# A hybrid Mamba-2 and attention step on Trainium2: operand parts tied behind the newest weight part

## The chip, the cores and the metric

The kernel runs on one core of a Trainium2 chip (trn2). The metric is the device time of one execution in microseconds (us). TensorE (PE) multiplies, VectorE (DVE), ScalarE (ACT) and GpSimd (POOL) do the elementwise work, and SyncE (SP) issues the DMAs between the memory of the chip and the on-chip buffers. Products are accumulated in PSUM banks and read from there by DVE or ACT.

## What is computed

The reference is one inference step of a two-layer decoder trunk. Eight sampled sequences of 8 tokens, one prompt of 1024 tokens and 16 meta tokens go through it together, 1104 columns in all; after the first layer the meta tokens are dropped and 1088 columns remain. Cut to what matters here:

```python
def sq_relu_mlp(h, norm_w, w_up, w_down):
    return h + jnp.square(jax.nn.relu(rmsnorm(h, norm_w) @ w_up)) @ w_down

# layer 0
out = gated_group_rmsnorm(y, z, gate_w) @ w_out      # the output product of the Mamba-2 mixer
h = h + out
h = sq_relu_mlp(h, mlp_norm_w[0], w_up[0], w_down[0])
# layer 1
h = h + swa(queries(h), shared keys and values) @ w_o
h = sq_relu_mlp(h, mlp_norm_w[1], w_up[1], w_down[1])
y = rmsnorm(h, final_norm_w)
```

The model is 1024 wide, the mixer's inner width is 2048 and the MLP's is 4096. All of it is float32.

## The kernel before

**Split operands.** A float32 product is made of three matmuls in the type fp32r (`mm3`, L205 to L207): high part of the weight by high part of the operand, high by low, and low by high. So every operand of PE is first split in two parts: ACT writes the high part with a cast, then DVE writes the low part as a difference. A pair of such instructions is called parts below. There are three places that make them in the stages of this case:

- `wparts` (L1051) makes weight parts. It takes a tile from a ring of six (`wtile`, tag w), casts on ACT (L1053) and subtracts on DVE (L1054). Its source is a weight block as loaded (raw) or a sum of such blocks (s), made on DVE (L1172 and L1178 in the output and down products, L1063 and L1069 in the up product).
- `parts` in `side_io` (L1223) makes the parts of one side, an operand of a product set, in place: ACT L1235, DVE L1236. The tiles are pieces of the big buffers S and R and a few of their own called A.
- `block_parts` (L1148) makes a quarter of the parts of a plain block, the buffer R0 (tile R): ACT L1151, DVE L1152.

**The stages.** The output product (in the trace from about 850 to 985 us), the up product and the down product of each layer (up 1100 to 1380 us and 2225 to 2505 us, down 1437 to 1699 us and 2560 to 2819 us) use a scheme of seven products in place of eight for 2 by 2 blocks. The mixer and the attention lie before and between them and are not touched.

**block_products (L1239)** runs the output product in 2 blocks and each down product in 4. In a block it takes four sets p = 0 to 3, and in a set seven products i = 0 to 6. One product is 18 matmuls of 128 x 276 columns (272 in layer 1) into one of four PSUM banks ma, mb, mc, md, in the order that CHAIN gives (`"adcbacd"` in even sets, `"abcdacb"` in odd ones). The products of a set accumulate on one another in their banks, and after each of the seven an eviction on DVE (L1270) adds the bank to one of the tiles us and hh; the first set's first is a copy on ACT (L1289). A bank can be written anew only when its eviction has read it, and a weight tile of the ring only when the product that used it six weights before is done. In the last block of a stage three more additions of us to hh follow (L1294), two of them on POOL and one on DVE.

The nested `step(b, p, i)`, called after each product, loads and splits the operands to come: the first two sides of block b + 1 after product 2 of sets 1 and 2, the other five at the positions that `make` lists, from set 3 into set 0 of the next block, and in the last block the four quarters of the plain block, after product 2 of sets 1, 2 and 3 and product 5 of set 3 (`last[1]`, which is `block_parts`). The stage then ends with a plain block product that reads R0.

**up (L1123)** runs 14 pairs f = 2 to 15 of the up product (`up_pair`) with weights from `up_weights` and sides that are made once at its start; it loads R0 at f = 8 and splits its quarters after f = 12 to 15, for the plain block with which the down product begins.

**What sets the order.** The order in which the code is traced is not the order on the engines. A scheduler places each engine's instructions by a simulated time, under the data dependences; it may put an instruction that was traced late ahead of one traced before it on the same engine. The context manager `tc.issue_after(ins)` adds an edge that only orders: what is traced inside it stands behind `ins` on the engine of `ins`. The kernel before uses it in two places, behind the newest load of weights (`last_raw`; one is `load_stream`, L1139).

Of the kernel before, what the change touches and what calls it, by code (L numbers as in the profile page):

```python
# [3 lines left out]

# [5 lines left out]
F32 = mybir.dt.float32  # L10
F32R = mybir.dt.float32r
AF = mybir.ActivationFunctionType
ALU = mybir.AluOpType
# [81 lines left out]
class Stream:  # L95
# [29 lines left out]
    def load(self, X):  # L125

        self.X = X
        for c in self.rs:
            self.k.nc.sync.dma_start(out=X[:, :, self.cols(c)], in_=self.h_d[:, :, self.cols(c)])
        for c in list(self.rs):  # L130
            self.norm(c)
# [11 lines left out]
class Kernel:  # L143
# [906 lines left out]
    def wparts(self, src, shape):  # L1050
        nc = self.nc  # L1051
        t = self.wtile([P, 2] + shape)
        nc.scalar.copy(out=t[:, 0], in_=src)  # L1053
        nc.vector.tensor_tensor(out=t[:, 1], in0=src, in1=t[:, 0].bitcast(F32), op=ALU.subtract)  # L1054
        return t[:, 0], t[:, 1]

    def up_weights(self, layer, f):
# [90 lines left out]
    def block_parts(self, j, buf):  # L1148
        nc = self.nc
        hi, lo = buf[:, 0, j], buf[:, 1, j]  # L1150
        nc.scalar.copy(out=hi, in_=lo.bitcast(F32))  # L1151
        nc.vector.tensor_tensor(out=lo, in0=lo.bitcast(F32), in1=hi.bitcast(F32), op=ALU.subtract)  # L1152

    def down_block(self, layer, b, buf, hts, chs, tail=0, done=None, step=None):

# [83 lines left out]
    def block_products(self, w, big, us, slots, load, parts, free, make, last, more, early=(0, 0), w0=None):  # L1239


        nc = self.nc
        nn = us.shape[2]
        qw = nn // 2
        nb = len(slots)
        h = [[big[:, 4 * j:4 * j + 4, i * nn:i * nn + nn] for i in range(2)] for j in range(2)]

        def step(b, p, i):

            if b == nb - 1:  # L1250
                if (p, i) == (0, 0):
                    last[0]()
                if p > 0 and i == 2:
                    last[1](p - 1)
                if p == 3 and i == 5:
                    last[1](3)
            else:
                for k in range(2):
                    if i == 0 and p == early[k]:
                        load(b + 1, k)  # L1260
                if p in (1, 2) and i == 2:
                    parts(b + 1, p - 1)
                if p == 3 and i in free[b]:
                    load(b + 1, free[b].index(i) + 2)
                if p == 3 and i in make[b]:
                    parts(b + 1, make[b].index(i) + 2)
            if p == 0 and b and i + 7 in make[b - 1]:
                parts(b, make[b - 1].index(i + 7) + 2)

        tt = lambda out, x, y: nc.vector.tensor_tensor(out=out, in0=x, in1=y, op=ALU.add)  # L1270
        for b in range(nb):
            for p in range(4):
                banks = {}
                hv = [[h[j][i][:, p] for i in range(2)] for j in range(2)]
                uv = us[:, p]
                for i, (wh, wl) in enumerate(w0 if w0 is not None and (b, p) == (0, 0) else self.down_weights(w[b], p)):
                    e = self.CHAIN[p % 2][i]
                    new = e not in banks
                    if new:
                        banks[e] = self.pq.tile([P, 1024], F32, tag=e, bufs=1, name="m" + e)  # L1280
                    x = [(hi[:, q], lo[:, q]) for hi, lo in slots[b][i] for q in range(lo.shape[1])]
                    for k in range(2):
                        cs = slice(k * qw, k * qw + qw)
                        self.mm3(banks[e][:, 512 + (k - 1) * qw:512 + k * qw], [(wh[:, q], wl[:, q]) for q in range(KB)],
                                 [(hi[:, cs], lo[:, cs]) for hi, lo in x], new)
                    pv = banks[e][:, 512 - qw:512 + qw]
                    to = (uv, hv[1][1], hv[1][1], uv, hv[0][0], hv[1][0], hv[0][1])[i]
                    if i == 0 and b == 0:
                        nc.scalar.copy(out=uv, in_=pv)  # L1289
                    else:  # L1290
                        tt(to, pv, to)
                    if b == nb - 1 and i in (3, 4, 5):
                        e, to = ((nc.gpsimd, hv[1][1]), (nc.gpsimd, hv[0][1]), (nc.vector, hv[1][0]))[i - 3]
                        e.tensor_tensor(out=to, in0=to, in1=uv, op=ALU.add)  # L1294
                    step(b, p, i)
                    more(b, p, i)
# [736 lines left out]
```

## Time and profile before

| | us |
|---|---|
| median of 3 runs | 2892.56 |
| the runs | 2887.66, 2892.56, 2895.99 |
| the profiled execution, its own time | 2889.1 |
| its span, first to last instruction | 2887.0 |
| mean granted clock of PE | 0.991 |

| engine | busy us | share of the span |
|---|---|---|
| PE | 2805.9 | 97% |
| DVE | 2084.4 | 72% |
| ACT | 1417.7 | 49% |
| POOL | 465.4 | 16% |

A line of the trace names the engine, the line of the program, the operation and the tiles, out<-in. The name of a tile leaves out its buffer number, so `w<-s,w` is the low part of a weight made of a sum and its high part, `S<-S` or `A<-A` are side parts, `R<-R` are plain parts at L1152 and side parts at L1236, and `us<-ma,us` is an eviction of the bank ma. DVE's instructions overlap a little at their ends: a row of 0.55 us may be followed 0.47 us after its start.

Matmuls of one product follow one another without a gap when nothing is waited for, so a stretch of PE shows its losses in two ways: as waits with a releaser, and as fewer matmuls in a stretch than in a quiet one of the same length. Where the granted clock is below 1.00, matmuls are slower too.

### The profile page before, as it was taken

What the parts mean: (1) busy time and instruction counts of PE and PEld (TensorE: products, weight loads), DVE (VectorE), ACT (ScalarE), POOL (GpSimd) and SP (SyncE); (2) the same over time, 40 slices, a digit from 0 to 9 for tenths busy, and PEclk for the clock granted to TensorE, in tenths of its full rate; (3) what the DMA queues carried; (4) which work ended last, traced back from release to release, by engine and by line L of the source; (5) the groups of instructions that cost most, each with busy time, mean ns of one, the idle gap of its engine ahead of it and who ended that gap; (6) DMA issues with size and microseconds to landing.
All of it is one profiled execution on the core that took longest, in us unless ns stands there. A gap on an engine that the chain in (4) does not pass through costs nothing.

```text
span 2887.0 us, 51424 instructions
## 1 busy us (share of the span) xinstructions
PE 2805.9 (97%) x19895; PEld 2700.3 (94%) x19895; DVE 2084.4 (72%) x3615; ACT 1417.7 (49%) x2742; POOL 465.4 (16%) x659
## 2 busy tenths in 40 slices
PE   8999999989999999999999999999999999999997
PEld 6999999979989999999999999888989999999997
DVE  6788888876778686665677875676688666567786
ACT  6555555555654275454343336556555454523333
POOL 3255555551100100000000022110110000000011
PEclk9999999999999999999999999999999999999999
DMA  4244444457654225343645423456553444624431
GB/s 138 83 128 124 123 123 126 129 134 259 247 200 162 93 92 175 128 149 142 250 171 188 163 94 103 162 170 235 184 191 126 138 146 147 231 101 132 146 102 69
DMA packets 219467, 433.41 MB, mean 150 GB/s; under 512 B 30728, under 2 KB 128392, under 8 KB 216648
## 3 DMA queue, kind: packets, MB, share of 16 engines
q1 hardware_dynamic: 219224, 430.14, 44.9%
q8 instruction: 156, 2.56, 0.4%
q14 instruction: 87, 0.71, 0.1%
HBM read 302.71 MB, written 128.32 MB: 149 GB/s over the span
## 4 chain that ended last, share of the span: by engine, by line
PE 82%; DVE 8%; DMA 4%; ACT 2%; issue 2%; POOL 0%; SPq 0%; DVEq 0%; ACTq 0%; POOLq 0%
PE g L205 11%; PE g L206 11%; PE g L207 11%; PE mc L205 4%; PE mc L207 4%; PE mc L206 4%; PE ma L205 3%; PE ma L206 3%; PE ma L207 3%; PE md L206 3%; PE md L207 3%; PE md L205 3%; PE mb L205 3%; PE mb L207 3%; PE mb L206 3%
## 5 line engine op out<-in xcount | busy, mean ns | idle before, releaser
L206 PE MATMUL g<-S,w 128*128 128x384 f32 (+2 forms) x1584 | 531.6, 336 | 0.0
L205 PE MATMUL g<-S,w 128*128 128x384 f32 (+2 forms) x1584 | 529.8, 335 | 1.9 <-DMA w<-ws_q 0.7
L207 PE MATMUL g<-S,w 128*128 128x384 f32 (+2 forms) x1584 | 527.4, 333 | 0.0
L1053 ACT CAST w<-s 128x384 fp32r<-128x384 f32 (+1 forms) x272 | 150.4, 557 | 346.4 <-DVE s L1178 85.3
L205 PEld LDWEIGHTS g<-S,w 128*128 128x128 f32 x1584 | 298.7, 189 | 4.5 <-issue 1.2
L206 PEld LDWEIGHTS g<-S,w 128*128 128x128 f32 x1584 | 298.8, 189 | 3.0 <-issue 2.4
L207 PEld LDWEIGHTS g<-S,w 128*128 128x128 f32 x1584 | 299.4, 189 | 2.2 <-issue 1.7
L1294 POOL TENSOR_TENSOR hh<-hh,us 128x552 f32<-128x552 f32 (+1 forms) x24 | 36.3, 1532 | 1563.4 <-DVE us L1270 1563.4
L205 PE MATMUL ma<-S,w 128*128 128x276 f32 (+1 forms) x808 | 234.7, 291 | 5.9 <-DVE us L1270 4.4
L207 PE MATMUL ma<-S,w 128*128 128x276 f32 (+1 forms) x808 | 234.4, 290 | 0.0
L206 PE MATMUL ma<-S,w 128*128 128x276 f32 (+1 forms) x808 | 234.0, 290 | 0.0
L1054 DVE TENSOR_TENSOR w<-s,w 128x384 fp32r<-128x384 f32 (+1 forms) x272 | 167.1, 619 | 69.3 <-ACT w L1053 69.2
L1053 ACT CAST w<-raw 128x384 fp32r<-128x384 f32 (+1 forms) x204 | 111.8, 556 | 162.7 <-PE mc L207 47.2
L171 ACT CAST w<-raw 128x1024 fp32r<-128x1024 f32 x96 | 100.6, 1048 | 133.6 <-PE g L206 49.0
L205 PEld LDWEIGHTS ma<-S,w 128*128 128x128 f32 x808 | 153.1, 189 | 7.2 <-ACT w L1053 3.6
L206 PE MATMUL g<-R,w 128*128 128x384 f32 (+2 forms) x480 | 158.3, 330 | 0.0
L205 PE MATMUL g<-R,w 128*128 128x384 f32 (+2 forms) x480 | 157.8, 329 | 0.0
L207 PE MATMUL g<-R,w 128*128 128x384 f32 (+2 forms) x480 | 157.7, 329 | 0.0
L172 DVE TENSOR_TENSOR w<-raw,w 128x1024 fp32r<-128x1024 f32 x96 | 122.6, 1277 | 43.9 <-ACT w L171 29.3
L206 PEld LDWEIGHTS ma<-S,w 128*128 128x128 f32 x808 | 153.2, 190 | 0.1
L207 PEld LDWEIGHTS ma<-S,w 128*128 128x128 f32 x808 | 152.9, 189 | 0.0
L205 PE MATMUL mc<-S,w 128*128 128x276 f32 (+1 forms) x512 | 148.1, 289 | 0.3 <-DVE hh L1270 0.3
(491 smaller groups left out, 8568.4 us busy)
## 6 DMA issues: line engine op xcount, KB each, us to landing
raw<-in_w_up_dram SPq DMA_DIRECT2D x64, 512.0 KB
raw<-in_w_in_dram SPq DMA_DIRECT2D x48, 512.0 KB
raw<-in_w_downs_dram SPq DMA_DIRECT2D x64, 384.0 KB
w<-ws_o SPq DMA_DIRECT2D x48, 512.0 KB
w<-ws_q SPq DMA_DIRECT2D x40, 512.0 KB
ab<-acs_d SPq DMA_DIRECT2D x64, 256.0 KB
S<-t_d SPq DMA_DIRECT2D x18, 828.0 KB
S<-t_e SPq DMA_DIRECT2D x18, 816.0 KB
```

Source lines behind the costliest of these rows:

```text
L171: nc.scalar.copy(out=wh, in_=raw)
L172: nc.vector.tensor_tensor(out=wl, in0=raw, in1=wh.bitcast(F32), op=ALU.subtract)
L205: mm(out=out, lhsT=wh, rhs=xh, start=(first and k == 0), stop=False)
L206: mm(out=out, lhsT=wh, rhs=xl, start=False, stop=False)
L207: mm(out=out, lhsT=wl, rhs=xh, start=False, stop=(k == n - 1))
L1053: nc.scalar.copy(out=t[:, 0], in_=src)
L1054: nc.vector.tensor_tensor(out=t[:, 1], in0=src, in1=t[:, 0].bitcast(F32), op=ALU.subtract)
L1294: e.tensor_tensor(out=to, in0=to, in1=uv, op=ALU.add)
```

## The change

`wparts` now keeps its two instructions as `last_hi` (ACT) and `last_lo` (DVE), those of the newest weight parts traced. A new context manager `behind` opens `issue_after` on both. `block_parts` always works inside it, and so do the three calls of `parts` in the `step` of `block_products`. So each of these operand parts stands, on ACT and on DVE, behind the weight parts that were traced last before it. The calls of `parts` outside `step` (in `gates_out`, and in `first` of `down_blocks`) are left as they were. No instruction is added, taken away or given other data.

```diff
-        nc.scalar.copy(out=t[:, 0], in_=src)
-        nc.vector.tensor_tensor(out=t[:, 1], in0=src, in1=t[:, 0].bitcast(F32), op=ALU.subtract)
+        self.last_hi = nc.scalar.copy(out=t[:, 0], in_=src).ins
+        self.last_lo = nc.vector.tensor_tensor(out=t[:, 1], in0=src, in1=t[:, 0].bitcast(F32), op=ALU.subtract).ins
         return t[:, 0], t[:, 1]
...
     def block_parts(self, j, buf):
         nc = self.nc
         hi, lo = buf[:, 0, j], buf[:, 1, j]
-        nc.scalar.copy(out=hi, in_=lo.bitcast(F32))
-        nc.vector.tensor_tensor(out=lo, in0=lo.bitcast(F32), in1=hi.bitcast(F32), op=ALU.subtract)
+        with self.behind():
+            nc.scalar.copy(out=hi, in_=lo.bitcast(F32))
+            nc.vector.tensor_tensor(out=lo, in0=lo.bitcast(F32), in1=hi.bitcast(F32), op=ALU.subtract)
+
+    @contextmanager
+    def behind(self):
+
+        with self.tc.issue_after(self.last_hi), self.tc.issue_after(self.last_lo):
+            yield
...
                 if p in (1, 2) and i == 2:
-                    parts(b + 1, p - 1)
+                    with self.behind():
+                        parts(b + 1, p - 1)
                 if p == 3 and i in free[b]:
                     load(b + 1, free[b].index(i) + 2)
                 if p == 3 and i in make[b]:
-                    parts(b + 1, make[b].index(i) + 2)
+                    with self.behind():
+                        parts(b + 1, make[b].index(i) + 2)
             if p == 0 and b and i + 7 in make[b - 1]:
-                parts(b, make[b - 1].index(i + 7) + 2)
+                with self.behind():
+                    parts(b, make[b - 1].index(i + 7) + 2)
```

In the changed program the lines from `block_parts` on have higher numbers: the plain parts are at L1152 and L1153, the sums at L1179 and L1185, the side parts at L1242 and L1243, and the evictions at L1280.

More of the change, by code (lines that the diff above doesn't have):

```diff
@@ L1 @@
-from contextlib import ExitStack
+from contextlib import ExitStack, contextmanager
 from functools import partial
```

## The prediction

> **What bounds the kernel now.** I read the page first. Its engine line says whose time counts.
>
> ```profile
> PE 2805.9 (97%) x19895; PEld 2700.3 (94%) x19895; DVE 2084.4 (72%) x3615; ACT 1417.7 (49%) x2742; POOL 465.4 (16%) x659
> ```
>
> TensorE (PE) is busy for 97% of the span of 2887.0 us, and the change leaves its matmuls as they are. So it can win only where PE stands still or runs at a low clock. Next come PE's waits over the whole run: tile and line, released by whom, us in total, times, the longest.
>
> ```profile
> PE mb L205 <- DVE us L1270: 5.9, 4, 1.7
> ...
> PE md L205 <- ACT w L1053: 5.2, 2, 3.2
> PE mb L207 <- DVE w L1054: 4.4, 2, 2.8
> PE ma L205 <- DVE us L1270: 4.4, 4, 1.7
> PE md L206 <- DVE S L1236: 4.3, 2, 2.3
> ...
> PE mb L205 <- DVE hh L1270: 1.9, 2, 1.0
> ...
> PE ma L205 <- ACT S L1235: 0.9, 1, 0.9
> ...
> PE ma L205 <- ACT w L1053: 0.6, 1, 0.6
> ```
>
> These are the waits of the product stages (banks ma to md), 27.6 us. PE waits there for an eviction (us, hh), a weight part (w) or an operand part (S), nearly all from VectorE (DVE). Taken window by window, they lie where one block of products gives way to the next. The windows of these places, and two quiet stretches after them (columns: length, busy us of PE, PEld, DVE, ACT and POOL with their instructions, granted clock, DMA):
>
> ```profile
> 852.00:868.00 16.00, 12.90 (x84) 12.13 (x83) 16.00 (x19) 9.14 (x11) 0.00 (x0) 0.89 0.57 221
> 920.00:940.00 20.00, 16.34 (x126) 15.89 (x125) 20.00 (x28) 6.30 (x10) 3.04 (x2) 1.00 0.16 54
> 1495.00:1515.00 20.00, 17.28 (x129) 16.29 (x129) 20.00 (x27) 7.53 (x11) 0.00 (x0) 1.00 0.32 105
> 1565.00:1585.00 20.00, 17.94 (x140) 17.56 (x139) 19.17 (x27) 7.06 (x11) 0.00 (x0) 1.00 0.28 92
> 1632.00:1652.00 20.00, 15.88 (x108) 15.17 (x107) 19.37 (x26) 5.73 (x8) 3.02 (x2) 0.91 0.17 60
> 2620.00:2640.00 20.00, 16.78 (x130) 16.18 (x129) 19.70 (x29) 6.67 (x11) 0.00 (x0) 1.00 0.18 61
> 2688.00:2708.00 20.00, 16.64 (x129) 16.04 (x128) 19.69 (x29) 6.16 (x11) 0.00 (x0) 1.00 0.19 53
> 2752.00:2772.00 20.00, 17.20 (x123) 16.86 (x123) 19.97 (x27) 8.30 (x12) 2.73 (x2) 0.91 0.29 101
> 945.00:985.00 40.00, 40.00 (x317) 40.00 (x316) 29.22 (x42) 9.43 (x16) 8.95 (x6) 1.00 0.15 50
> 2640.00:2680.00 40.00, 40.00 (x321) 40.00 (x320) 25.31 (x43) 11.53 (x19) 0.00 (x0) 1.00 0.41 133
> ```
>
> In the quiet rows a matmul takes 40.00/317 = 0.126 us (layer 0) and 40.00/321 = 0.125 us (layer 1). Length less matmuls times that is what a place loses, low clock included: 5.4, 4.1, 3.7, 2.3, 6.4, 3.8, 3.9 and 4.7 us, together 34.3. At each DVE is busy throughout (19.2 to 20.0 of 20), while in the quiet rows it has 11 to 15 us of 40 free. DVE is thus a bound for some 15 us at a time: work taken out of these bursts is worth its length up to PE's loss there, and where it goes instead there is room.
>
> **The change, part by part.** No instruction is added or taken away; each tied part now stands behind the newest weight part on ACT and on DVE. What this moves, first on DVE in layer 1's down product, block 0 to block 1. The trace there:
>
> ```profile
> 2626.00 0.72 DVE L1270 TENSOR_TENSOR us<-ma,us 128x544 f32<-128x544 f32 x1
> 2626.64 0.71 DVE L1270 TENSOR_TENSOR hh<-md,hh 128x544 f32<-128x544 f32 x1
> 2627.27 1.85 DVE L1236 TENSOR_TENSOR A<-A 128x1632 fp32r<-128x1632 f32 x1
> 2629.03 0.55 DVE L1054 TENSOR_TENSOR w<-s,w 128x384 fp32r<-128x384 f32 x1
> 2629.50 0.55 DVE L1054 TENSOR_TENSOR w<-raw,w 128x384 fp32r<-128x384 f32 x1
> 2629.97 1.85 DVE L1236 TENSOR_TENSOR A<-A 128x1632 fp32r<-128x1632 f32 x1
> 2631.74 1.02 DVE L1054 TENSOR_TENSOR w<-s,w 128x384 fp32r<-128x384 f32 x2
> 2632.68 0.72 DVE L1270 TENSOR_TENSOR us<-mb,us 128x544 f32<-128x544 f32 x1
> ```
>
> DVE before, the same place (us and hh are evictions of products, w weight parts, s sums of weights; A_27469 and A_27470 are operands of block 2, a whole block ahead of their use):
>
> ```order
> L1270 TENSOR_TENSOR us<-ma,us 128x544
> L1270 TENSOR_TENSOR hh<-md,hh 128x544
> L1236 TENSOR_TENSOR A_27469<-A_27469 128x1632
> L1054 TENSOR_TENSOR w<-s,w 128x384
> L1054 TENSOR_TENSOR w<-raw,w 128x384
> L1236 TENSOR_TENSOR A_27470<-A_27470 128x1632
> L1054 TENSOR_TENSOR w<-s,w 128x384 x2
> L1270 TENSOR_TENSOR us<-mb,us 128x544
> ```
>
> DVE now (its L1243 and L1280 are before's L1236 and L1270):
>
> ```order
> L1280 TENSOR_TENSOR us<-ma,us 128x544
> L1054 TENSOR_TENSOR w<-s,w 128x384
> L1280 TENSOR_TENSOR hh<-md,hh 128x544
> L1054 TENSOR_TENSOR w<-raw,w 128x384
> L1054 TENSOR_TENSOR w<-s,w 128x384 x2
> L1280 TENSOR_TENSOR us<-mb,us 128x544
> L1280 TENSOR_TENSOR hh<-mc,hh 128x544
> L1243 TENSOR_TENSOR A_27469<-A_27469 128x1632
> ```
>
> Both A parts now stand behind the eviction us<-mb, one by a row, the other by a product set. Start to start they take 1.76 and 1.77 us, so us<-mb can come 3.5 us earlier, and the wait mb <- us (at most 1.7) goes. The rows ahead of us<-ma stay, two side parts among them, so ma <- us (4.4) stays wherever only A parts move. The same two parts leave at four transitions (windows 1495, 1565, 2620, 2688): 5.9 us by the waits row, and the 0.6 of ma <- w, which ends behind the same burst. Each wait costs a restart too: window 920 loses 4.1 with two waits of 4.4 − 2.8 = 1.6 and 4.3 − 2.3 = 2.0, that is 0.25 each. So 6.5 + 4 × 0.25 = 7.5 us. Bounds: 0.8, if only the second transition gains, and the four windows' whole loss, 13.7.
>
> At the last transition of each stage (windows 920, 1632, 2752) the four plain parts of the last block (R) leave too. DVE before, layer 1:
>
> ```order
> L1236 TENSOR_TENSOR A_27469<-A_27469 128x1632
> L1270 TENSOR_TENSOR us<-md,us 128x544
> L1152 TENSOR_TENSOR R_24141<-R_24141 128x1088
> L1054 TENSOR_TENSOR w<-s,w 128x384
> L1152 TENSOR_TENSOR R_24141<-R_24141 128x1088
> L1270 TENSOR_TENSOR hh<-ma,hh 128x544
> L1236 TENSOR_TENSOR A_27470<-A_27470 128x1632
> L1178 TENSOR_TENSOR s<-s,raw 128x384
> L1054 TENSOR_TENSOR w<-s,w 128x384
> L1270 TENSOR_TENSOR hh<-mc,hh 128x544
> L1152 TENSOR_TENSOR R_24141<-R_24141 128x1088 x2
> ```
>
> DVE now, from the next product set's first side part on:
>
> ```order
> L1243 TENSOR_TENSOR S<-S 128x1632
> L1280 TENSOR_TENSOR us<-ma,us 128x544
> L1243 TENSOR_TENSOR S<-S 128x1632
> L1280 TENSOR_TENSOR hh<-md,hh 128x544
> L1054 TENSOR_TENSOR w<-s,w 128x384
> L1054 TENSOR_TENSOR w<-raw,w 128x384
> L1243 TENSOR_TENSOR S<-S 128x1632
> L1054 TENSOR_TENSOR w<-s,w 128x384
> L1280 TENSOR_TENSOR hh<-mc,hh 128x544
> L1280 TENSOR_TENSOR us<-mb,us 128x544
> L1054 TENSOR_TENSOR w<-s,w 128x384
> L1153 TENSOR_TENSOR R_24141<-R_24141 128x1088
> ```
>
> The R parts are gone from ahead of the side parts; the first stands now behind us<-mb, the others a set apart each. But the third S has two more weight parts ahead of it. The trace:
>
> ```profile
> 2747.04 1.28 DVE L1152 TENSOR_TENSOR R<-R 128x1088 fp32r<-128x1088 f32 x1
> ...
> 2748.71 1.28 DVE L1152 TENSOR_TENSOR R<-R 128x1088 fp32r<-128x1088 f32 x1
> ...
> 2753.88 2.48 DVE L1152 TENSOR_TENSOR R<-R 128x1088 fp32r<-128x1088 f32 x2
> ...
> 2758.32 1.85 DVE L1236 TENSOR_TENSOR S<-S 128x1632 fp32r<-128x1632 f32 x1
> 2760.09 0.55 DVE L1054 TENSOR_TENSOR w<-s,w 128x384 fp32r<-128x384 f32 x1
> ...
> 2762.76 3.62 DVE L1236 TENSOR_TENSOR S<-S 128x1632 fp32r<-128x1632 f32 x2
> ```
>
> Four R parts at 1.20 (2753.88 plus 2.48, two of them) are 4.8 us. In window 1632 PE's waits add to 4.1:
>
> ```profile
> PE md L206 <- DVE S L1236: 2.3, 1, 2.3
> PE mb L205 <- DVE hh L1270: 1.0, 1, 1.0
> PE ma L205 <- DVE us L1270: 0.8, 1, 0.8
> ```
>
> That is less than 4.8, so they go, and with them the clock's drop (0.91 over 20 us is 1.8 us). I take 6.1 of the 6.4; low bound 3.0 (the S wait and little of the clock). Window 920: 1.6 + 2.0 = 3.6, bounds 1.8 and 4.1. Window 2752 loses 4.7 to the weight part (2.8) and the clock (1.8). There the third S would end at 2766.4 − 4.8 + 2 × 0.47 = 2762.5, where PE reads it in
>
> ```profile
> 2766.71 0.29 PE L206 MATMUL md<-S,w 128*128 128x272 f32 x1
> ```
>
> less 4.7, at 2762.0: a new wait of 0.5, or 1.2 with one eviction (0.7) more ahead. I take 1.2, so 3.5 remain, bounds 2.0 and 4.7. Whether low clock goes with the stalls is weighed by the rows: 1.00 where the longest single stall is 2.0 (window 920), 0.91 where it is 2.3 or 2.8. [...]
>
> Two more places. Window 852 waits for side parts that stay in order (0.9, then 2.0 on a weight): 0, bounds 0 and 2.0. At layer 1's up product PE's wait of 3.2 on a weight stays in kind, but ten norm matmuls now come ahead of it, 10 × 0.125 = 1.2; bounds 0 and 1.7.
>
> What hides the moved parts: in the last block DVE has 10.8 of 40 us free (row 945) and needs 1.2 for an R part once in a set of 16 us; an A part's 1.8 falls in a row as quiet. ACT is busy for at most 9.1 us in these windows, POOL's order is unchanged, SP issues the same DMAs with 14 of 855 rows moved (a DMA share of 0.16 to 0.57 here leaves room), and the R parts of the up products, which move from their start to their last four pairs, still come over two products ahead of their first reader. Without that cover each of the 12 R parts in last blocks would cost 1.2.
>
> Sum: 7.5 + 6.1 + 3.6 + 3.5 + 1.2 = 21.9 us; lowest 0.8 + 3.0 + 1.8 + 2.0 = 7.6, highest 13.7 + 6.4 + 4.1 + 4.7 + 1.7 + 2.0 = 32.6. The profiled execution took 2889.1 us, 2.1 of it outside the span, so it would take 2867.2. The median of the runs is 3.5 higher: 2892.6 − 21.9 = 2870.7.
>
> **The rivals.** (a) The burst is conserved: DVE does the same work near the same place, and a wait that goes comes back an eviction later. For it: ma <- us stays, and DVE is full through each window. Against it: the free 11 to 15 us in the rows after. Some 2 us would be left: 2890.6.
>
> (b) The R parts collide with POOL. In the last block POOL adds hh and us (L1294) just behind us<-mb, where the first R part now stands:
>
> ```profile
> 933.29 3.04 POOL L1294 TENSOR_TENSOR hh<-hh,us 128x552 f32<-128x552 f32 x2 [150.87 <-DVE us L1270]
> ```
>
> DVE beside it:
>
> ```profile
> 933.77 1.32 DVE L1054 TENSOR_TENSOR w<-s,w 128x384 fp32r<-128x384 f32 x1
> ...
> 935.65 1.10 DVE L1178 TENSOR_TENSOR s<-s,raw 128x384 f32<-128x384 f32 x1
> ```
>
> Such parts take 0.55 elsewhere. At worst each of the 12 R parts loses a whole POOL add, 1.5, and all reaches PE: 18 us, leaving 3.9, so 2888.7. Against it: DVE's free time there. [...]
>
> (c) Slower: an operand part comes too late. Tied behind a weight part, it also waits for that part's place in the ring of six, which PE frees; PE then waits for its own operand as in md <- S. That wait costs 2.3, with the clock 1.8 more, 4.1. It decides from 4.4 us at each of the seven transitions on (30.6 in all, against 21.9); with 5.0 it is 35 − 21.9 = 13 us slower, 2906. Against it: parts stand four products, some 9 us, ahead of their readers.
>
> (d) The low clock stays in windows 1632 and 2752 for reasons of its own: 3.6 less, 2874.3. [...]
>
> That the ties do nothing is out: the order shows the moves.
>
> **How the numbers follow.** Forecast 0.69, (a) 0.13, (b) 0.05, (c) 0.06, (d) 0.07. A measurement here tells 0.3% (8.7 us) from no change; so faster 0.69 + 0.07 = 0.76, within 0.13 + 0.05 = 0.18, slower 0.06. The range starts at the sum's upper bound rounded, 2861 (2892.6 − 32), and reaches up to 2889 to take in (b), leaving out (a) and (c), 0.19.
>
> **What would show it.** Right: PE's waits lose the row mb <- us wholly, md <- S falls from 4.3 to about 1, ma <- us stays near 3.6, windows 1632 and 2752 have clock 1.00, and DVE shows an R part beside POOL's adds with PE unmoved. Wrong: new waits of PE on S, A, or w in the second product set of a block; R parts of over 2.5 us with PE waiting behind; or the eight windows together still losing over 25 us.

## The result, and the profile after

The changed kernel takes 2868.03 us (median of four runs, 2865.23 to 2871.14), the kernel before 2892.65 (four runs): 24.6 us less, ratio 0.9919 with a 95% interval of 0.9906 to 0.9932. The forecast was 21.9 us less, 2870.7. The profiled execution took 2865.23 us, its span 2863.5, which is 23.5 less than the span before.

The engine line of the page after, with the same columns as before:

```profile
PE 2798.5 (98%) x19895; PEld 2695.8 (94%) x19895; DVE 2080.8 (73%) x3615; ACT 1419.9 (50%) x2742; POOL 471.1 (16%) x659
```

The number of instructions is the same on every engine. PE is busy for 7.4 us less; it ran at half clock for 45.5 us of this execution and for 56.3 us of the one before. POOL is busy for 5.7 us more, which comes back below. PE's waits over the run after, the rows of the product stages (tile and line, released by whom, us in total, times, the longest):

```profile
PE ma L205 <- DVE us L1280: 3.2, 2, 1.9
...
PE md L205 <- ACT w L1053: 3.0, 2, 2.7
...
PE md L206 <- DVE S L1243: 1.8, 2, 1.3
...
PE ma L206 <- DVE S L1243: 1.4, 1, 1.4
...
PE ma L205 <- ACT S L1242: 1.2, 1, 1.2
...
PE mb L206 <- DVE S L1243: 0.4, 1, 0.4
```

They add to 11.0 us, where the rows before added to 27.6. The rows mb <- us (5.9), mb <- w (4.4) and mb <- hh (1.9) are gone; md <- S has gone from 4.3 to 1.8. One row is new, ma <- S (L206, 1.4), at the start of the output product. The windows of the same eight places, moved to where they now lie (length, busy us of PE, PEld, DVE, ACT and POOL with their instructions, granted clock, DMA):

```profile
848.00:864.00 16.00, 12.74 (x94) 11.87 (x94) 13.53 (x17) 9.71 (x12) 0.00 (x0) 1.00 0.75 298
914.00:934.00 20.00, 18.71 (x147) 18.48 (x147) 19.36 (x25) 10.25 (x13) 4.51 (x2) 1.00 0.32 115
1479.00:1499.00 20.00, 20.00 (x160) 20.00 (x159) 18.96 (x24) 12.93 (x15) 0.00 (x0) 1.00 0.82 309
1547.00:1567.00 20.00, 20.00 (x159) 20.00 (x158) 20.00 (x27) 11.00 (x12) 0.00 (x0) 1.00 0.66 243
1612.00:1632.00 20.00, 20.00 (x160) 20.00 (x158) 19.88 (x26) 9.07 (x12) 3.25 (x2) 1.00 0.57 214
2604.00:2624.00 20.00, 18.69 (x149) 18.50 (x149) 18.73 (x29) 5.56 (x10) 0.00 (x0) 1.00 0.30 86
2668.00:2688.00 20.00, 18.12 (x133) 17.93 (x132) 19.18 (x30) 5.97 (x10) 0.00 (x0) 0.91 0.22 66
2732.00:2752.00 20.00, 19.50 (x156) 19.28 (x155) 19.37 (x28) 8.69 (x12) 4.32 (x2) 1.00 0.32 119
```

Read as in the prediction (length less matmuls times 0.126 us in layer 0 and 0.125 in layer 1) they lose 4.2, 1.5, 0, 0, 0, 1.4, 3.4 and 0.5, together 11.0, where they lost 34.3. That is 23.3 of the 23.5 us of the span. The lengths of the stages agree. From its first to its last matmul in the banks ma to md, the output product took 138.1 us before and takes 134.2 now, the down product of layer 0 269.1 and 256.2, that of layer 1 265.8 and 258.9, the two up products 297.9 and 301.3, now 297.9 and 300.9. Together that is 24.1 less, and everything else takes 0.6 more.

But look at the third number of busy time: DVE is still busy for 18.7 to 20.0 of 20 us at the transitions, in the three middle rows too, where PE loses nothing. The burst did not become shorter in a window of 20 us; what changed is what in it stands ahead of what PE waits for. In layer 1's down product, from block 0 to block 1, DVE now runs so (start, us, line, operation, tiles):

```profile
2609.09 0.72 DVE L1280 TENSOR_TENSOR us<-ma,us 128x544 f32<-128x544 f32 x1
2609.72 0.55 DVE L1054 TENSOR_TENSOR w<-s,w 128x384 fp32r<-128x384 f32 x1
2610.19 0.72 DVE L1280 TENSOR_TENSOR hh<-md,hh 128x544 f32<-128x544 f32 x1
2610.82 0.55 DVE L1054 TENSOR_TENSOR w<-raw,w 128x384 fp32r<-128x384 f32 x1
2611.29 1.02 DVE L1054 TENSOR_TENSOR w<-s,w 128x384 fp32r<-128x384 f32 x2
2612.23 0.72 DVE L1280 TENSOR_TENSOR us<-mb,us 128x544 f32<-128x544 f32 x1
2612.87 0.72 DVE L1280 TENSOR_TENSOR hh<-mc,hh 128x544 f32<-128x544 f32 x1
2613.50 1.85 DVE L1243 TENSOR_TENSOR A<-A 128x1632 fp32r<-128x1632 f32 x1
```

From us <- ma to us <- mb it is 3.14 us now, 6.68 before: the two A parts, 3.5 us, as worked out.

### The profile page after: what moved, and what is told of

Its sections match the earlier page's. It is cut to its first block, busy times and chain, and to the rows that moved or that the text cites. A ratio compares the mean times of both kernels' runs of the same rounds, so it can differ in the third digit from the quotient of the medians.

```text
span 2863.5 us, 51417 instructions
## 1 busy us (share of the span) xinstructions
PE 2798.5 (98%) x19895; PEld 2695.8 (94%) x19895; DVE 2080.8 (73%) x3615; ACT 1419.9 (50%) x2742; POOL 471.1 (16%) x659
## 4 chain that ended last, share of the span: by engine, by line
PE 89%; DVE 5%; DMA 3%; ACT 2%; issue 1%; SPq 0%; POOL 0%; DVEq 0%; ACTq 0%; POOLq 0%
PE g L206 12%; PE g L205 12%; PE g L207 12%; PE ma L205 4%; PE mc L205 4%; PE mc L207 4%; PE ma L206 4%; PE ma L207 4%; PE mc L206 4%; PE md L206 3%; PE md L207 3%; PE md L205 3%; PE mb L206 3%; PE mb L207 3%; PE mb L205 3%; PE y L665 1%
## 5 line engine op out<-in xcount | busy, mean ns | idle before, releaser
L206 PE MATMUL g<-S,w 128*128 128x384 f32 (+2 forms) x1584 | 531.1, 335 | 0.0
L206 PEld LDWEIGHTS g<-S,w 128*128 128x128 f32 x1584 | 298.5, 188 | 3.0 <-issue 2.4
L1304 POOL TENSOR_TENSOR hh<-hh,us 128x552 f32<-128x552 f32 (+1 forms) x24 | 42.7, 1802 | 1530.4 <-DVE us L1280 1530.4
L206 PE MATMUL ma<-S,w 128*128 128x276 f32 (+1 forms) x808 | 233.9, 289 | 1.4 <-DVE S L1243 1.4
L206 PE MATMUL g<-R,w 128*128 128x384 f32 (+2 forms) x480 | 158.4, 330 | 0.0
L206 PEld LDWEIGHTS ma<-S,w 128*128 128x128 f32 x808 | 152.8, 189 | 1.6 <-DVE S L1243 1.6
```

The source lines that it names most:

```text
L206: mm(out=out, lhsT=wh, rhs=xl, start=False, stop=False)
```

## Experiments

All times below are medians of four to seven runs. The kernel before was run beside each group: 2888.59 us for the first (plain_only to evict_tie), 2888.84 for the second (changed_again to plain_left_out), 2892.12 for the third (the last three). The changed kernel took 2868.03 in the first comparison and 2868.36 in the second group; beside the third it was not run. Gains are told against the kernel before of the same group. By that measure the changed kernel gains 24.6 in the first comparison and 20.5 in the second group. PE's waits are those of the product stages, from the waits view of each profile; a dash means no row over 0.25 us. (In plain_left_out mb waits for the high part of a weight from ACT, elsewhere in that column for the low part from DVE.)

| kernel | us | ratio to before, interval | mb <- us | ma <- us | mb <- w | md <- S |
|---|---|---|---|---|---|---|
| before | 2892.65 | | 5.9 | 4.4 | 4.4 | 4.3 |
| changed | 2868.03 | 0.9919 (0.9906 to 0.9932) | – | 3.2 | – | 1.8 |
| plain_only | 2877.00 | 0.9958 (0.9946 to 0.9971) | 4.7 | 4.0 | – | 0.3 |
| sides_only | 2881.24 | 0.9975 (0.9964 to 0.9986) | – | 3.4 | 4.3 | 4.3 |
| up_untied | 2868.20 | 0.9929 (0.9917 to 0.9942) | – | 3.4 | – | 0.5 |
| evict_tie | 2863.41 | 0.9911 (0.9896 to 0.9926) | 0.3 | – | – | – |
| changed_again | 2868.36 | 0.9927 (0.9915 to 0.9940) | – | 3.9 | – | 1.3 |
| evict_tie_again | 2863.69 | 0.9913 (0.9901 to 0.9925) | – | – | – | – |
| late_sides | 2864.90 | 0.9911 (0.9898 to 0.9925) | – | – | – | – |
| plain_left_out | 2875.09 | 0.9951 (0.9938 to 0.9963) | 5.7 | 3.5 | 0.9 | 0.7 |
| pool_on_dve | 2864.91 | 0.9909 (0.9896 to 0.9923) | – | 3.1 | – | 2.4 |
| plain_later | 2868.38 | 0.9917 (0.9903 to 0.9930) | – | 3.5 | – | 2.2 |
| evict_plain_later | 2862.83 | 0.9901 (0.9887 to 0.9914) | 0.4 | – | – | – |

**One half of the change at a time.** First the plain parts alone:

```diff
-                    with self.behind():
-                        parts(b + 1, p - 1)
+                    parts(b + 1, p - 1)
...
-                    with self.behind():
-                        parts(b + 1, make[b].index(i) + 2)
+                    parts(b + 1, make[b].index(i) + 2)
...
-                with self.behind():
-                    parts(b, make[b - 1].index(i + 7) + 2)
+                parts(b, make[b - 1].index(i + 7) + 2)
```

> Only block_parts is tied (the R parts of the last blocks and of the up products); the side parts are free as in the kernel before. Theory (length of the DVE burst at each transition): the gain is that of the three last transitions of the stages alone. The changed kernel lost 2.7, 6.6 and 4.0 us less there than before, and 0.5 less at layer 1's up product, together 13.8, so 2892.6 - 13.8 = 2879 us, ratio 0.995; the four waits mb <- us (5.9 us) stay. Rival (one kind of part is enough, the rest is granted clock that fell otherwise): 2868 to 2872, or no change at 2892.

Measured 2877.00, 11.6 us under before, where 13.8 were expected. Its waits:

```profile
PE md L205 <- ACT w L1053: 5.2, 2, 3.2
...
PE mb L205 <- DVE us L1277: 4.7, 4, 1.6
PE ma L205 <- DVE us L1277: 4.0, 3, 1.8
...
PE md L206 <- DVE S L1243: 0.3, 1, 0.3
```

mb <- w is gone and md <- S nearly, those of the last transitions; the four waits mb <- us stay. Then the side parts alone:

```diff
-        with self.behind():
-            nc.scalar.copy(out=hi, in_=lo.bitcast(F32))
-            nc.vector.tensor_tensor(out=lo, in0=lo.bitcast(F32), in1=hi.bitcast(F32), op=ALU.subtract)
+        nc.scalar.copy(out=hi, in_=lo.bitcast(F32))
+        nc.vector.tensor_tensor(out=lo, in0=lo.bitcast(F32), in1=hi.bitcast(F32), op=ALU.subtract)
```

> Only the side parts are tied, block_parts is free as in the kernel before. Theory (length of the DVE burst): the gain is that of the transitions at which A parts leave, 3.9 + 2.5 + 2.4 + 0.5 = 9.3 us, so 2883 us, ratio 0.997; mb <- us goes, while md <- S (4.3) and mb <- w (4.4) stay at the last transitions. Its gain and that of the plain parts alone add up to the whole change's 24.6 within 3 us. Rival (the two are not independent, a shorter burst at one place moves its wait to the next): the sum is under 18 or over 31.

Measured 2881.24, 7.4 us under before, where 9.3 were expected. Its waits are the mirror image, mb <- us gone and the two of the last transitions as before:

```profile
PE mb L207 <- DVE w L1054: 4.3, 3, 2.7
PE md L206 <- DVE S L1242: 4.3, 2, 2.3
PE ma L205 <- DVE us L1279: 3.4, 3, 1.7
```

The two gains add to 19.0, which is outside the 3 us around 24.6 that were expected, and not far from the 18 of the rival. But beside this group the kernel before took 4 us less, and the whole change there (up_untied, next) gains 20.4. The profiles put the sum on the other side: there the five product stages are 15.6 us shorter in plain_only, 12.1 in sides_only and 23.9 in up_untied. So the halves add up to within 4 us. Each ends its own waits and leaves the other's, except that the wait mb <- hh of the last transition in layer 0 (1.0) goes with either.

The order of the instructions in the built programs tells a little more: of the three calls of `parts` in `step`, only the one after product 2 of sets 1 and 2 (the A parts) moves anything. With that call alone tied, the program has the order of sides_only on every engine, and with only the two calls that go by `make` tied it has the order of the kernel before. Those parts stood behind their weights already.

**The up products.**

```diff
-                    self.block_parts(f - 12, R0)
+                    self.block_parts(f - 12, R0, False)
...
-        with self.behind():
+        with self.behind() if tie else ExitStack():
```

> The whole change, but the R parts of the two up products are free again. Theory: PE loses nothing in the up products either way, so the time is that of the changed kernel within 0.1%, 2868 us, with at most 0.5 us back at layer 1's up product (wait md <- w 3.2 again in place of 2.7). Rival (those parts count, as they stand in the up product's start where ACT and DVE make weights): 2871 or more.

Measured 2868.20, the changed kernel's time within 0.2 us. Moving the eight R parts of the up products is worth nothing that can be measured. The wait at layer 1's up product is 2.7 here, as in the changed kernel, and not 3.2 again as expected; it is 2.7 in sides_only too, 3.2 in plain_only, and with the eviction tie 3.2 again. So the 0.5 us gained there came with the ties of the side parts, not with these R parts.

**The side parts behind the newest eviction.** What the changed kernel has left in layer 1's down product is ma <- us, behind two side parts.

```diff
-                with self.behind():
+                with self.behind(), self.tc.issue_after(self.last_ev):
                     parts(b, make[b - 1].index(i + 7) + 2)
...
-                        tt(to, pv, to)
+                        self.last_ev = tt(to, pv, to).ins
```

> The whole change, and the side parts made in set 0 stand also behind the newest eviction traced, so us <- ma comes ahead of two side parts in the burst. Theory (length of the DVE burst ahead of the eviction): the two waits ma <- us that the changed kernel has left in layer 1's down product (3.2 us, with restarts and one low-clock window 5) go: 2863 us. Rival (an operand part comes too late): PE waits for S parts at the transitions, 1 to 2 us at each of seven, and the time is 2868 to 2880.

Measured 2863.41, then, beside the changed kernel on one chip:

> The changed kernel itself once more, beside the next three on the same chip. Theory and rival alike: 0.992 of the time before; it gives the spread of the places from run to run (the transition in the output product lost 1.6 us in the first profile and 0.3 in the kernel with the up products untied, whose order there is the same).

> The kernel with the set 0 side parts behind the newest eviction once more, for its difference from the changed kernel on one chip. Theory (the two waits ma <- us of layer 1's down product were all that was left there): 4 to 5 us under the changed kernel, and the profile loses under 0.6 us at each of the three transitions of that stage. Rival (the first comparison was spread from the mixer and the attention): the same as the changed kernel within 2 us.

2868.36 and 2863.69: 4.7 us. The three transitions of layer 1's down product in the second profile of the eviction tie:

```profile
2600.00:2620.00 20.00, 20.00 (x162) 20.00 (x161) 20.00 (x27) 10.76 (x14) 0.00 (x0) 1.00 0.49 182
2664.00:2684.00 20.00, 20.00 (x161) 20.00 (x161) 19.62 (x28) 8.96 (x13) 0.00 (x0) 1.00 0.40 147
2728.00:2748.00 20.00, 20.00 (x161) 19.85 (x160) 20.00 (x28) 9.73 (x14) 6.01 (x2) 1.00 0.44 158
```

161 or 162 matmuls in 20 us are PE's full rate (321 in 40 before). DVE is busy for 19.6 to 20.0 us of each window and PE feels none of it. So it is the order inside the burst that makes the loss, and not how full DVE is.

**An operand that comes late.** To the eviction tie was added:

```diff
-        make = [(3, 4, 6, 7, 9), (3, 4, 6, 7, 9), (3, 4, 7, 8, 10)]
+        make = [(3, 4, 6, 9, 10), (3, 4, 6, 9, 10), (3, 4, 7, 9, 10)]
```

and in the output product 9 in place of 8.

> The same, with the last two sides of each block made one or two products later in the code, so that each stands one eviction further back on DVE, the last of them behind us <- mb. Theory of the operand that comes too late: PE now waits for its own S part at the transitions, 1 to 2 us at each of the seven, 7 to 14 us over the kernel with the eviction tie, which would put it near 2875. Rival (there are still two products between a part and its reader): no more than 2 us over it, 2865.

Measured 2864.90, 1.2 us over the eviction tie, with no wait on S at any of the seven transitions. The rival holds: with the last side part behind us <- mb the parts still come before their readers. So the forecast's slower case (c) was not near.

**The plain parts left out.** From the kernel before; the plain product at the end of these stages then reads unsplit data:

```diff
-                            (lambda: self.block_load(rd, 3, R0), lambda j: self.block_parts(j, R0)), more, (1, 1),
+                            (lambda: self.block_load(rd, 3, R0), lambda j: None), more, (1, 1),
...
-                            (lambda: self.block_load(rd, 7, R0), lambda j: self.block_parts(j, R0)), step)
+                            (lambda: self.block_load(rd, 7, R0), lambda j: None), step)
```

> The kernel before, with nothing tied; it leaves out the splitting of the plain block in the last block of the three stages (the 12 R parts on ACT and on DVE; the plain product that follows reads unsplit data). Theory (an R part costs by standing in the burst, and nothing where it stands now): the gain of the plain parts' ties alone, 11.6 us, within 2 us. Rival (where they stand now they cost something, on DVE or beside POOL): leaving them out gains more, up to 12 x 1.2 = 14 us on top.

Measured 2875.09, 13.8 us under before; the ties on the same parts gain 11.6. The 2.2 between them is just over the 2 us of the expectation, and the two intervals overlap (0.9938 to 0.9963, 0.9946 to 0.9971). Twelve R parts in their new places thus cost some 2 us, if anything, far from the 14 of the rival.

**POOL beside the R parts.** In the changed kernel two R parts are longer than the others, 2.05 and 2.04 us. The spread of L1153 (shortest, median, longest in ns), then one of the two long ones with the POOL additions beside it, the first alone and then both:

```profile
L1153 DVE TENSOR_TENSOR R<-R x20: 1279/1298/2053, 928.9 to 2781.2; 128x1104 fp32r<-128x1104 f32 x12, 128x1088 fp32r<-128x1088 f32 x8
```

```profile
958.36 2.05 DVE L1153 TENSOR_TENSOR R<-R 128x1104 fp32r<-128x1104 f32 x1 [0.36 <-ACT R L1152]
```

```profile
957.62 1.63 POOL L1304 TENSOR_TENSOR hh<-hh,us 128x552 f32<-128x552 f32 x1 [12.34 <-DVE us L1280]
```

```profile
957.62 4.04 POOL L1304 TENSOR_TENSOR hh<-hh,us 128x552 f32<-128x552 f32 x2 [12.34 <-DVE us L1280]
```

Before, this pair of additions took 2.96. At the first place where the two engines meet, the R part has its usual length and POOL alone is slower, 4.51 where the first pair took 3.04 before:

```profile
928.94 1.30 DVE L1153 TENSOR_TENSOR R<-R 128x1104 fp32r<-128x1104 f32 x1
```

```profile
928.63 4.51 POOL L1304 TENSOR_TENSOR hh<-hh,us 128x552 f32<-128x552 f32 x2 [144.75 <-DVE us L1280]
```

```profile
L1304 POOL TENSOR_TENSOR hh<-hh,us 128x552 f32<-128x552 f32 (+1 forms) x24 | 42.7, 1802 | 1530.4 <-DVE us L1280 1530.4
```

So the collision of the forecast's case (b) is there, and mostly POOL pays for it: 42.7 − 36.3 (the group before) = 6.4 us in all. Two evictions on DVE now wait for such an addition, 1.3 us together. Does PE? One kernel takes POOL out of it, one moves the R parts away:

```diff
-                        e, to = ((nc.gpsimd, hv[1][1]), (nc.gpsimd, hv[0][1]), (nc.vector, hv[1][0]))[i - 3]
+                        e, to = ((nc.vector, hv[1][1]), (nc.vector, hv[0][1]), (nc.vector, hv[1][0]))[i - 3]
```

> The changed kernel with the 24 additions of us to hh (L1304) moved from POOL to DVE, so that no R part stands beside POOL. Theory (POOL and DVE take turns there, but PE does not feel it): no R part is over 1.4 us (two are 2.05 in the changed kernel), DVE gets 24 x 0.72 = 17 us more work in the last blocks, and the time stays that of the changed kernel within 0.2%, 2868 us. Rival (the turn-taking reaches PE): up to 3 us faster than the changed kernel. A third case: DVE's 17 us more are felt, 2 to 8 us slower.

```diff
-                if p > 0 and i == 2:
+                if p > 0 and i == 5:
                     last[1](p - 1)
-                if p == 3 and i == 5:
+                if p == 3 and i == 6:
                     last[1](3)
```

> The changed kernel with the plain block's quarters made three products later in the code (after product 5 in place of 2, the last after 6), so that the first R part stands half a set behind us <- mb, away from POOL's additions. Theory (DVE has room there either way): the POOL additions fall from 42.7 back to about 36.3 us in all, the time stays that of the changed kernel within 0.2%. Rival (the place beside POOL costs PE something): 2 to 4 us faster.

Without POOL, 2864.91: the longest R part is 1.32 us, and 24 more additions on DVE cost nothing. It is 3 us under the changed kernel, which is the rival's number, but its ratio's interval (0.9896 to 0.9923) overlaps the changed kernel's, and the product stages show no gain: together they take 1249.2 us in its profile, 1248.1 and 1247.0 in the two profiles of the changed kernel. The 3 us do not come from where the R parts stand. With the R parts moved away, 2868.38: no R part is over 1.31 us, POOL's additions take 37.8, and the time is the changed kernel's. PE does not feel the collision. Nor does it in the second profile of the eviction tie, where POOL's eight additions of layer 1's stage take 19.1 us (14.2 in the changed kernel) and PE waits at none of the seven transitions.

**Both moves together** (eviction tie and later plain parts).

> The kernel with the eviction tie and the later quarters of the plain block together, a try for the best version. Theory: that of the eviction tie alone within 0.2%, about 25 us under before (ratio 0.9912), since nothing is lost any more in the stages where R parts stand. Rival: the two add to something, 27 to 29 us under before.

Measured 2862.83, 29.3 us under before of that group. By that number the rival holds, but the kernel before took 3.3 us more in this group than in the second. Within the group it is 5.5 us under plain_later, where the eviction tie was 4.7 under the changed kernel, and its time is within 1 us of the eviction tie's 2863.41 and 2863.69. So the later plain parts add nothing that these runs can tell. By its median it is the fastest kernel here, and the eviction tie alone is as good.

## Why the prediction was right

The order of DVE came out as the prediction had read it, and with it the waits. The gain lies on both sides of the forecast of 21.9: 24.6 in the first comparison, 20.4 in the first group (up_untied) and 20.5 in the second (changed_again).

**The transitions with A parts** (forecast 7.5). The four windows lost 13.7 and now lose 0 + 0 + 1.4 + 3.4 = 4.8: 8.9 gained. The mechanism, us <- mb out from behind the two A parts, is shown by the rows above, by the missing row mb <- us, and by sides_only. That the size is near has some luck in it: by the waits, 3.7 of the 7.5 belonged to layer 0 and 3.8 to layer 1, and the gains were 6.0 and 2.9. The low bound of 0.8 is not worked out from a row; the second transition alone waited 1.4 and 0.6.

Two things differ. In layer 0 all of the loss went, although "ma <- us stays wherever only A parts move" was the argument; this was wrong there and right in layer 1 (3.2 left). The side parts themselves came earlier in layer 0. Their first cast on ACT waited for its load:

```profile
1482.35 0.51 ACT L1053 CAST w<-raw 128x384 fp32r<-128x384 f32 x1 [1.31 <-issue]
1486.61 1.58 ACT L1235 CAST S<-S 128x1656 fp32r<-128x1656 f32 x1 [3.75 <-DMA S<-t_d]
```

and after:

```profile
1477.12 0.51 ACT L1053 CAST w<-raw 128x384 fp32r<-128x384 f32 x1 [1.31 <-issue]
1479.16 1.58 ACT L1242 CAST S<-S 128x1656 fp32r<-128x1656 f32 x1 [1.52 <-DMA S<-t_d]
```

From the weight's cast to the side's it was 4.26 us and is 2.04; the whole burst starts that much sooner against PE. It is 1.76 in sides_only and 3.37 in plain_only, so this goes with the ties of the side parts. The prediction gave SP's moved rows no effect. That they are the reason for the earlier landing is likely but was not tried by itself.

The other difference: the second transition of layer 1 gained 0.5, where 1.7 for its wait and 0.25 for the restart were counted, since a low clock came there that the kernel before did not have (window 2668, 0.91).

**The last transitions** (forecast 6.1 + 3.6 + 3.5 = 13.2). They lost 6.4 + 4.1 + 4.7 and now lose 0 + 1.5 + 0.5: gains of 6.4, 2.6 and 4.2, together 13.2. plain_only alone gains 11.6, and in it mb <- w goes and md <- S nearly. That the sum is exact is luck, since the three terms miss by 0.3, 1.0 and 0.7. The new wait on the third S part that was foreseen for layer 1 is there, 0.5 long in this profile and 1.0 in the second one, and not 1.2. In the output product the prediction left no such wait; it is 1.3 in this profile and 0.3 in the second, and there is none in up_untied, whose order there is the same.

**The other two places.** For window 852, the start of the output product, the forecast was 0, since its side parts "stay in order". They do among themselves, but two weight casts now stand ahead of the fourth of them on ACT. The wait on the weight fell from 2.0 to 0.3, and a wait on that side part of 1.4 came, here and in every kernel with tied side parts; the sum of the waits stayed (3.1 before, 3.3 now). The window gained 1.2 only because the low clock did not come in this one profile. It came in the other twelve profiles of this case, that of the kernel before included (granted clock 0.86 to 0.93 from 845 to 870 us, 1.00 here), and in the second profile of the changed kernel the place lost 16.00 − 85 × 0.126 = 5.3, as before:

```profile
851.00:867.00 16.00, 13.12 (x85) 12.25 (x84) 13.23 (x16) 9.80 (x12) 0.00 (x0) 0.89 0.76 298
```

So 0 was the right size, for a reason that was in part wrong. At layer 1's up product 1.2 was forecast; the wait went from 3.2 to 2.7, so 0.5.

**The sum.** 8.9 + 13.2 + 1.2 + 0.5 = 23.8 against a forecast of 21.9, and 23.5 in the span. One reading of the waits before was too strong: of the 27.6 us "nearly all from DVE", 6.7 were released by ACT. The sum does not use it.

**The rivals.** (a), the conserved burst: its premise is true, DVE is as full at the transitions as it was, but its conclusion is not, since what is late now (an A part, an R part) has no reader for many products. (b): the collision is real, PE does not feel it. (c): late_sides shows room to spare. (d), a low clock with reasons of its own in windows 1632 and 2752: these places have clock 1.00 now, in both profiles of the changed kernel, and the low clock is still there in sides_only (0.97 from 1600 to 1660 us, 0.98 from 2720 to 2800), where the waits of 2.3 and 2.7 stay. So it hung on the stalls.

## What to carry to other kernels

When an engine is full for a while around a change of stage, ask of each of its instructions when its result is read. One that is read a block later, and stands ahead of an eviction that the bottleneck waits for now, costs the bottleneck a wait (here 1.2 to 1.7 us for two A parts of 3.5), even if the engine is no less busy when it is moved. Where a scheduler orders by data dependences alone, an edge that only orders, behind the newest thing that is urgent (here a weight part, better still an eviction), is a cheap way to move it; then look in the order which of the edges move anything.

## What the runs showed of the hardware

The low clock can follow a stall that is shorter than itself: in the changed kernel one of 1.88 us brought 3.41 us of it. It comes in stretches of 3.41, 6.83 or 10.24 us, on a grid of 3.41 (in the traces of the kernel before and of the changed one; only the stretch at the end of each has another length). PE waited so (the timeline, with what it was idle for in brackets):

```profile
2675.46 0.37 PE L205 MATMUL ma<-S,w 128*128 128x272 f32 x1 [1.88 <-DVE us L1280]
```

Three neighbouring stretches of 3.41 us there, with the columns of the windows above:

```profile
2673.28:2676.70 3.42, 1.54 (x13) 1.35 (x12) 3.42 (x5) 1.97 (x2) 0.00 (x0) 1.00 0.42 120
2676.70:2680.11 3.41, 3.41 (x17) 3.41 (x17) 3.41 (x6) 0.00 (x0) 0.00 (x0) 0.50 0.00 0
2680.11:2683.52 3.41, 3.41 (x29) 3.41 (x29) 3.41 (x7) 0.93 (x2) 0.00 (x0) 1.00 0.00 0
```

PE was busy for 1.54 of 3.42 us in the first, and the next ran 17 matmuls in place of 29. In the second profile of the same kernel a longer wait,

```profile
2613.70 0.36 PE L205 MATMUL ma<-S,w 128*128 128x272 f32 x1 [2.17 <-DVE us L1280]
```

fell across the border of two such stretches, and no low clock followed:

```profile
2609.49:2612.90 3.41, 2.05 (x17) 1.83 (x15) 3.41 (x4) 1.45 (x3) 0.00 (x0) 1.00 0.50 150
2612.90:2616.31 3.41, 2.60 (x21) 2.63 (x22) 3.41 (x8) 0.64 (x1) 0.00 (x0) 1.00 0.20 76
2616.31:2619.73 3.42, 3.42 (x29) 3.42 (x29) 3.42 (x5) 0.06 (x1) 0.00 (x0) 1.00 0.00 0
```

So half clock followed a stretch in which PE was idle for just over half (1.88 of 3.42), and none followed one with 1.36 of 3.41. The thirteen profiles of this case agree, counted stretch by stretch on the grid, without the first 30 and the last 20 us and from stretches at full clock: after one in which PE was idle for 1.9 us or more, half clock followed in 57 of 57 cases, after 1.3 to 1.9 us in 24 of 53, after 0.9 to 1.3 us in 3 of 73. By an estimate from the rows above, a wait of about 2 us in this kernel therefore costs either its length or some 1.5 us more (12 matmuls fewer at 0.125 us), by where it falls.

The other finding is the pair of R part and POOL addition. In both places above one of the two took longer, by roughly what the other had still to run. The first POOL addition at 928.63 took 2.85 us where the same one took 1.38 before, 1.47 more, as if it had begun at 930.10, about when the R part ended (928.94 + 1.30). At 958.36 the POOL addition of 957.62 had 0.89 of its 1.63 us left when the R part began, and the R part lost 0.75 (2.05 in place of 1.30).
